# Channel mixers' norms: Newton steps by GpSimd, first guess in one operation on VectorE

## The chip, the cores and the metric

The kernel runs on one core of one Trainium2 chip. The metric is the device time of one execution in microseconds (us); lower is better. Three runs of the kernel before took 1862.06 to 1864.02 us, with a median of 1863.17.

## The reference

A decoder trunk of two layers on 512 tokens of width 1024, all in float32. Each layer is a channel mixer, a token mixer and a second channel mixer, each with a root-mean-square norm in front:

```
h = h + 0.5 * swiglu(rmsnorm(h, ffn_norm_a[i]), ...)
m = rmsnorm(h, mix_norm[i])
h = h + mla_mixer(m, ...)        # layer 0;  nsa_mixer(m, ...) in layer 1
h = h + 0.5 * swiglu(rmsnorm(h, ffn_norm_b[i]), ...)
...
def rmsnorm(x, g):
    y = x32 * lax.rsqrt(jnp.mean(x32 * x32, axis=-1, keepdims=True) + RMS_EPS)
    return y.astype(x.dtype) * g
def swiglu(x, w_gate, w_up, w_down):
    return (jax.nn.silu(x @ w_gate) * (x @ w_up)) @ w_down
```

A final norm stands behind the second layer. The hidden width of the channel mixers is 2816. The latent mixer norms its two latents as well, so there are four channel norms (called a0, b0, a1, b1 here, by layer and place), four others that go through the same code (in front of each token mixer, and of the two latents), and the final one, which has its own code.

## The kernel before

The residual h lies transposed in SBUF: eight tiles of 128 features by 512 tokens. Every product is made of three TensorE passes over a high and a low part of both operands: ScalarE rounds an operand to its high part (L205 in `split`, L176 for a weight slab that is loaded by `slab_ahead`), VectorE subtracts it from the operand for the low part (L206, L178). So each weight slab of 128 x 1024 goes from a DMA through ScalarE and then VectorE before TensorE can use it whole; two buffers named w hold slabs that are ready.

A channel mixer (`ffn`) does its first three hidden tiles f = 0, 1, 2 plainly: for each a gate product into pg and an up product into pu, of 48 matmuls of 256 columns each (L401 to L403: high by high, high by low, low by high, so that the first read of the slab's low part is the third matmul). Behind them the hidden tiles are made with fewer products, from sums of blocks: `combine` reads the residual (ScalarE makes a pair of y halves, L267; VectorE the sums u, L271 to L273; ScalarE and VectorE the parts named four, L205 and L206), and `wsums` makes sums of weight blocks (L372 to L376) and their parts wh and wl.

The norm's factor is not needed for the plain products: the gains are put into x, the products are begun, and the factor, one number for each token, is multiplied in behind the gate product. It is found while TensorE is busy with f = 0 and f = 1: the sums of squares are brought into a column of 128 x 4 (four matmuls pc, L311; in a0 by ScalarE's accumulators, L490), and `rsqrt` finds the inverse root on VectorE by a first guess from the bits of the number (L299, L300) and three Newton steps of three operations (L302 to L304), all on tiles of 128 x 4 in the tile named small. Each operation reads the one before it. Behind the column stand a warm-up of ScalarE's Silu on one of its numbers (L524), four transposes on TensorE that spread it over all partitions (pb, L323), a copy to the tile row (L527), and then the gates (L437 to L439).

The order of the instructions on each engine is not that of the code: the framework's scheduler sets it from its own estimate of when operands are ready, and each engine then works through its queue strictly in that order. GpSimd does not work at these places but for the last additions of squares (L289). `self.to_ffn` is set by `norm_begin` and is true for the four channel norms.

## Time and profile before

| | us |
|---|---|
| median of 3 runs (lowest, highest) | 1863.17 (1862.06, 1864.02) |
| the profiled execution | 1862.05 |
| its span, first to last instruction | 1860.3 |
| TensorE busy | 1845.7 |
| VectorE busy | 1507.4 |
| ScalarE busy | 1064.5 |
| GpSimd busy | 296.7 |

The mean TensorE clock that was granted is 0.999. In the profile PE is TensorE, PEld its weight loads, DVE VectorE, ACT ScalarE, POOL GpSimd and SP SyncE. Rows of a timeline begin with the start and the length in us; a bracket behind a row is the idle time of the engine ahead of it and what ended it. Rows of a group end with busy us, mean ns of one, and idle time ahead of them. A matmul's length is modelled and overlaps the next one's: one of 256 columns starts about 0.112 us behind the other.

The four channel norms' first guesses start at 25.05 (a0), 560.70 (b0), 889.30 (a1) and 1520.81 us (b1).

### The profile page before, as it was taken

The page shows a single profiled execution, that of the slowest core. Times are in us where ns is not written, and L with a number is a line of the kernel's source. Part 1 is how long each engine was busy: PE and PEld are TensorE (multiplying, and loading weights), DVE is VectorE, ACT ScalarE, POOL GpSimd, SP SyncE. Part 2 cuts the span into 40 slices and gives each one's busy share as a digit, 9 for nine tenths or more (in the row PEclk, how much of TensorE's full clock was granted, in tenths as well). Part 3 has the DMA queues.
Part 4 walks back from the last instruction along what each step waited for, and adds up shares of the span by engine and source line. Part 5 has one row for each costly group of instructions (what it writes and reads, how often), then busy time and mean ns, then how long its engine had stood idle before and what let it go on. Part 6 is the DMA issues. An engine that isn't in the chain of part 4 may idle for free.

```text
span 1860.3 us, 37031 instructions
## 1 busy us (share of the span) xinstructions
PE 1845.7 (99%) x14464; PEld 1763.4 (95%) x14464; DVE 1507.4 (81%) x2810; ACT 1064.5 (57%) x1997; POOL 296.7 (16%) x370
## 2 busy tenths in 40 slices
PE   9999999999999999999999999999999999999998
PEld 9999999888889999999999999988888889999997
DVE  8988886688779988886898888666878888888885
ACT  7555553567666555554655545446776865555554
POOL 0000000258830000001000000022666620000000
PEclk9999999999999999999999999999999999999999
DMA  6433331434433433322443332162433133433321
GB/s 238 132 108 103 103 92 48 117 105 103 114 123 112 119 103 109 110 73 72 138 118 110 109 106 81 45 183 82 108 108 103 40 118 116 121 104 107 103 78 69
DMA packets 84351, 196.64 MB, mean 106 GB/s; under 512 B 10944, under 2 KB 38464, under 8 KB 84176
## 3 DMA queue, kind: packets, MB, share of 16 engines
q1 hardware_dynamic: 81664, 191.34, 34.9%
q10 hardware_dynamic: 2512, 2.93, 0.5%
q8 instruction: 114, 1.87, 0.4%
q14 instruction: 61, 0.50, 0.1%
HBM read 178.44 MB, written 2.16 MB: 97 GB/s over the span
## 4 chain that ended last, share of the span: by engine, by line
PE 93%; DVE 3%; ACT 1%; issue 1%; POOL 1%; DMA 0%; ACTq 0%; POOLq 0%; DVEq 0%
PE pd L462 8%; PE pd L464 8%; PE pd L463 8%; PE px L386 6%; PE px L388 6%; PE px L387 5%; PE pg L386 4%; PE pg L388 4%; PE pg L387 4%; PE pq L386 4%; PE pq L388 4%; PE pq L387 4%; PE o L1337 2%; PE pt L1310 2%; PE po L197 2%; PE po L199 2%
## 5 line engine op out<-in xcount | busy, mean ns | idle before, releaser
L462 PE MATMUL pd<-ah,wd 128*128 128x256 f32 x1152 | 318.3, 276 | 0.0
L464 PE MATMUL pd<-ah,wd 128*128 128x256 f32 x1152 | 318.3, 276 | 0.0
L463 PE MATMUL pd<-al,wd 128*128 128x256 f32 x1152 | 318.3, 276 | 0.0
L289 POOL TENSOR_TENSOR s<-s,sq 128x512 f32<-128x512 f32 x38 | 54.7, 1441 | 1050.3 <-ACT sq L285 1050.3
L462 PEld LDWEIGHTS pd<-ah,wd 128*128 128x128 f32 x1152 | 216.3, 188 | 0.0
L464 PEld LDWEIGHTS pd<-ah,wd 128*128 128x128 f32 x1152 | 216.3, 188 | 0.0
L463 PEld LDWEIGHTS pd<-al,wd 128*128 128x128 f32 x1152 | 216.3, 188 | 0.0
L206 DVE TENSOR_TENSOR w<-wr,w 128x1024 fp32r<-128x1024 f32 x72 | 88.2, 1225 | 120.7 <-ACT w L205 120.4
L386 PE MATMUL px<-four,wh 128*128 128x256 f32 x608 | 168.4, 277 | 0.4 <-ACT wh L205 0.2
L388 PE MATMUL px<-four,wl 128*128 128x256 f32 x608 | 168.2, 277 | 0.2 <-DVE wl L206 0.2
L386 PE MATMUL pq<-four,wh 128*128 128x256 f32 x608 | 168.1, 276 | 0.2 <-ACT uq L556 0.2
L387 PE MATMUL px<-four,wh 128*128 128x256 f32 x608 | 168.0, 276 | 0.0
L388 PE MATMUL pq<-four,wl 128*128 128x256 f32 x608 | 167.9, 276 | 0.0
L387 PE MATMUL pq<-four,wh 128*128 128x256 f32 x608 | 167.9, 276 | 0.0
L468 DVE SCALAR_TENSOR_TENSOR h<-pd,h 128x512 f32<-128x512 f32 x216 | 148.3, 686 | 15.4 <-PE pd L464 15.2
L205 ACT ACTIVATE wd<-wdr 128x384 fp32r<-128x384 f32 x192 | 99.2, 519 | 103.8 <-issue 64.6
L176 ACT ACTIVATE w<-wr 128x1024 fp32r<-128x1024 f32 (+3 forms) x89 | 80.8, 908 | 87.5 <-PE pd L464 20.6
L206 DVE TENSOR_TENSOR wd<-wdr,wd 128x384 fp32r<-128x384 f32 x192 | 105.8, 553 | 20.1 <-ACT wd L205 20.0
L178 DVE TENSOR_TENSOR w<-wr,w 128x1024 fp32r<-128x1024 f32 (+3 forms) x75 | 78.3, 1044 | 50.0 <-ACT w L176 49.8
L728 ACT ACTIVATE p<-p,small 128x512 f32<-128x512 f32 (+2 forms) x192 | 106.9, 558 | 19.0 <-DVE small L727 15.3
L386 PEld LDWEIGHTS px<-four,wh 128*128 128x128 f32 x608 | 114.1, 188 | 1.0 <-ACT wh L205 0.4
L388 PEld LDWEIGHTS px<-four,wl 128*128 128x128 f32 x608 | 114.2, 188 | 0.6 <-DVE wl L206 0.6
(379 smaller groups left out, 6264.9 us busy)
## 6 DMA issues: line engine op xcount, KB each, us to landing
wr<-in_w_gu SPq DMA_DIRECT2D x93, 512.0 KB, 3.5
ru<-in_w_gu SPq DMA_DIRECT2D x76, 512.0 KB, 4.3
wdr<-in_w_down SPq DMA_DIRECT2D x192, 192.0 KB, 2.5
wr<-in_w_down SPq DMA_DIRECT2D x24, 256.0 KB, 2.6
wr<-in_mla_w_o SPq DMA_DIRECT2D x8, 512.0 KB, 3.4
th<-btab_d SPq DMA_DIRECT2D x16, 256.0 KB, 3.7
wr<-in_nsa_w_q SPq DMA_DIRECT2D x8, 512.0 KB, 3.8
wr<-in_nsa_w_o SPq DMA_DIRECT2D x8, 512.0 KB, 3.7
```

What stands on the lines that cost most here:

```text
L176: self.copied = nc.scalar.activation(wh[:, m], raw[:, m], AF.Copy)
L178: nc.vector.tensor_tensor(wl[:, m], raw[:, m], f32v(wh[:, m]), op=ALU.subtract)
L205: nc.scalar.activation(hi, src, AF.Copy)
L206: (nc.gpsimd if pool else nc.vector).tensor_tensor(lo, src, f32v(hi), op=ALU.subtract)
L386: mm(out, wh[:, p], xh, start=first and p == 0, stop=False, skip_group_check=True)
L387: mm(out, wh[:, p], xl, start=False, stop=False, skip_group_check=True)
L388: mm(out, wl[:, p], xh, start=False, stop=last and p == KP - 1, skip_group_check=True)
L462: nc.tensor.matmul(o, wh, xh, start=k == b0 and x == 0, stop=False, skip_group_check=True)
L463: nc.tensor.matmul(o, wh, xl, start=False, stop=False, skip_group_check=True)
L464: last = nc.tensor.matmul(o, wl, xh, start=False, stop=k == b1 - 1, skip_group_check=True)
L468: nc.vector.scalar_tensor_tensor(self.h[c], p, 0.5, self.h[c], op0=ALU.mult, op1=ALU.add)
L728: nc.scalar.activation(p_sb[:, :n], p_sb[:, :n], AF.Exp, bias=nm, scale=-1.0, accum_out=sm)
```

## The change

The first guess becomes one operation on VectorE for all eight norms: the bits, read as an integer, times -0.5, plus the constant. For the four channel norms the three Newton steps are done by GpSimd, which has no operation of the form that joins a scalar and two tensors here, so that each step is four operations in place of three. The other four norms keep their steps on VectorE.

```
     def rsqrt(self, y, v, t, psum, n):
         nc.vector.tensor_scalar(v, psum, 1.0 / n, EPS, op0=ALU.mult, op1=ALU.add)
-        self.newton(y, v, t)
+        nc.vector.tensor_scalar(y.bitcast(I32), v.bitcast(I32), -0.5, float(0x5F3759DF), op0=ALU.mult, op1=ALU.add)
+        (self.newton_pool if self.to_ffn else self.newton)(y, v, t)

     def newton(self, y, v, t):
         nc = self.nc
-        nc.vector.tensor_scalar(y.bitcast(I32), v.bitcast(I32), 1, None, op0=ALU.logical_shift_right)
-        nc.vector.tensor_scalar(y.bitcast(I32), y.bitcast(I32), -1.0, float(0x5F3759DF), op0=ALU.mult, op1=ALU.add)
         for _ in range(3):
             nc.vector.scalar_tensor_tensor(t, y, -0.5, v, op0=ALU.mult, op1=ALU.mult)
             nc.vector.tensor_tensor(t, t, y, op=ALU.mult)
             nc.vector.scalar_tensor_tensor(y, t, 1.5, y, op0=ALU.add, op1=ALU.mult)
+
+    def newton_pool(self, y, v, t):
+        e = self.nc.gpsimd
+        for _ in range(3):
+            e.tensor_tensor(t, y, y, op=ALU.mult)
+            e.tensor_tensor(t, t, v, op=ALU.mult)
+            e.tensor_scalar(t, t, -0.5, 1.5, op0=ALU.mult, op1=ALU.add)
+            e.tensor_tensor(y, y, t, op=ALU.mult)
```

Seven lines are added ahead of the rest, so L437 before is L444 in the changed kernel, L524 is L531, and so on. The scheduler orders the queues anew. Away from the eight norms' places, and from what follows a0 up to about 64 us, TensorE's order is the same as before; at three places the following moves matter.

ScalarE at a1: y are the halves that `combine` makes, four its parts, w a weight slab, gains<-small the Silu warm-up that reads the norm's column. Before:

```order
L176 ACTIVATE w<-wr 128x1024
L267 ACTIVATE y<-h_104,gains 128x512
L267 ACTIVATE y<-h_108,gains 128x512
L205 ACTIVATE wh<-s_11777 128x512
L205 ACTIVATE wd<-wdr 128x384 x2
L205 ACTIVATE four<-u 128x1024 x2
L176 ACTIVATE w<-wr 128x1024
L524 ACTIVATE gains<-small 128x1
```

And with the change:

```order
L176 ACTIVATE w<-wr 128x1024
L267 ACTIVATE y<-h_104,gains 128x512
L531 ACTIVATE gains<-small 128x1
L267 ACTIVATE y<-h_108,gains 128x512
L205 ACTIVATE wh<-s_11780 128x512
L205 ACTIVATE wd<-wdr 128x384
L205 ACTIVATE four<-u 128x1024
L205 ACTIVATE wd<-wdr 128x384
L205 ACTIVATE four<-u 128x1024
L176 ACTIVATE w<-wr 128x1024
```

The warm-up, which waits for the column, has moved ahead of the second y, two fours and the slab of the up product of f = 1. In b0 it has likewise moved ahead of one four and the slab of the gate product of f = 2, and in b1 ahead of a y, a four, a y and the slab of the up product of f = 1; in a0 it stands ahead of a y, a four and a slab.

TensorE in a0, where the products of f = 1 end and those of f = 2 begin; pb are the four transposes of the column. Before:

```order
L403 MATMUL pg<-x,w 128x256
L401 MATMUL pg<-x,w 128x256
L323 MATMUL pb<-ident,small 128x128 x4
L402 MATMUL pg<-x,w 128x256
L403 MATMUL pg<-x,w 128x256
```

And with the change:

```order
L409 MATMUL pu<-x,w 128x256
L410 MATMUL pu<-x,w 128x256
L330 MATMUL pb<-ident,small 128x128 x4
L408 MATMUL pg<-x,w 128x256
L409 MATMUL pg<-x,w 128x256
```

The transposes stood behind 28 matmuls of the gate product of f = 2, and now stand ahead of its first. In b0, a1 and b1 they stand where they stood.

VectorE behind the first guess of b0, where the first row is that guess:

```order
L295 TENSOR_SCALAR small<-small 128x4
L206 TENSOR_TENSOR wl<-ru,wh 128x1024
L178 TENSOR_TENSOR w<-wr,w 128x1024
L206 TENSOR_TENSOR four<-u,four 128x1024
L273 TENSOR_TENSOR u<-y,u 128x256
L206 TENSOR_TENSOR wl<-s_7371,wh 128x512
L206 TENSOR_TENSOR four<-u,four 128x1024
L178 TENSOR_TENSOR w<-wr,w 128x1024 x2
```

Before, the steps of Newton's method stood between these rows; now nothing of the norm does, and the second four is the one that reads ScalarE's four behind the warm-up.

## The prediction

> **What bounds the kernel now.** I read the page's busy table first, then the waits, then the stretches around two of the four places where a channel mixer's norm is worked out.

> ```profile
> PE 1845.7 (99%) x14464; PEld 1763.4 (95%) x14464; DVE 1507.4 (81%) x2810; ACT 1064.5 (57%) x1997; POOL 296.7 (16%) x370
> PE pb L323 <- DVE small L304: 1.0, 2, 0.6
> 22.00:36.00 14.00, 13.54 (x120) 13.37 (x119) 12.62 (x29) 13.24 (x21) 0.00 (x0) 1.00 0.73 255
> 886.00:908.00 22.00, 21.83 (x192) 21.63 (x192) 21.05 (x42) 14.80 (x21) 0.00 (x0) 1.00 0.58 182
> ```

> The columns of the stretches are PE, PEld, DVE, ACT and POOL busy. TensorE is the bound: any wait put into its queue is paid in full, and work taken off VectorE is worth only the TensorE waits that it ends. In the second row, the waits, all that TensorE is seen to lose to Newton's last step is 1.0 us, twice, at pb. At the norms GpSimd is idle while VectorE is 90 to 96% full: GpSimd is free there, but VectorE's queue leaves few gaps.

> **What is removed.** A Newton step on VectorE:

> ```profile
> L303 DVE TENSOR_TENSOR small<-small 128x4 f32<-128x4 f32 x24 | 3.8, 160 | 0.4
> 32.24 0.29 PE L323 MATMUL pb<-ident,small 128*128 128x128 f32 x1 [0.46 <-issue]
> 373.70 0.30 PE L323 MATMUL pb<-ident,small 128*128 128x128 f32 x1 [0.59 <-DVE small L304]
> ```

> Forty-four such instructions leave VectorE (10 at each of four channel norms, 1 at each of four other norms), 44 x 0.16 = 7.0 us of a queue that does not bound. Gain: the other norms' chains lose one dependent step of 0.16 plus about 0.04, so 0.2 us each; TensorE waits for three of them (373.70 above is the largest), and I count 0.5 us. The 0.46 us at 32.24 is the channel norm's own wait, replaced below.

> **What a step costs on GpSimd.** The nearest dependent small step is L1146, read by L1147:

> ```profile
> 1328.40 0.22 POOL L1146 TENSOR_TENSOR small<-small,gcmp 128x16 f32<-128x16 f32 x1
> 1328.70 1.05 POOL L1147 TENSOR_TENSOR e<-e,small 128x512 f32<-128x512 f32 x1
> ```

> From start to start 0.30 us, so twelve steps alone take 3.6 us. By the reported span alone it would be 12 x 0.22 = 2.6. [...]

> But it is not alone. Three pairs show GpSimd and VectorE keeping each other out:

> ```profile
> 1226.75 1.30 POOL L968 TENSOR_SCALAR btab<-tb 16x10 f32<-16x10 f32 x1
> 1226.75 1.23 DVE L178 TENSOR_TENSOR w<-wr,w 128x1024 fp32r<-128x1024 f32 x1 [5.01 <-ACT w L176]
> 1228.02 0.37 POOL L968 TENSOR_SCALAR btab<-tb 16x10 f32<-16x10 f32 x2
> 1505.87 1.72 DVE L178 TENSOR_TENSOR w<-wr,w 128x1024 fp32r<-128x1024 f32 x1
> 1507.37 1.38 POOL L289 TENSOR_TENSOR s<-s,sq 128x512 f32<-128x512 f32 x1 [0.86 <-ACT sq L285]
> 1507.51 1.78 DVE L209 SCALAR_TENSOR_TENSOR x<-h,ngains,x 128x512 fp32r<-128x512 f32 x1
> 1510.95 0.74 DVE L209 SCALAR_TENSOR_TENSOR x<-h,ngains,x 128x512 fp32r<-128x512 f32 x1
> ```

> The 16x10 operation of GpSimd, two of which take 0.37 us a little later, takes 1.30 and ends 0.07 us after VectorE's 1.23. In the second pair the roles are turned: L289 comes while L178 runs, gets in when that ends (1507.59), and L209 behind it, 0.74 us alone, takes 1.78. So a step that meets a VectorE operation on two SBUF tensors waits to its end, then goes ahead of the next; and by the time the dependent step is ready, 0.3 us on, that next one is running. While VectorE is full, GpSimd does one Newton step per VectorE operation, like the old interleaving. [...]

> **How long the chains get.** VectorE's operations at these places, all on two SBUF operands, grouped, and then the starts of a0's first and of L299 in each place:

> ```profile
> L206 DVE TENSOR_TENSOR four<-u,four 128x1024 fp32r<-128x1024 f32 x3 | 3.6, 1221 | 1.5 <-ACT four L205 1.5
> L178 DVE TENSOR_TENSOR w<-wr,w 128x1024 fp32r<-128x1024 f32 x2 | 2.4, 1220 | 0.0
> L271 DVE TENSOR_TENSOR u<-y 128x512 f32<-128x512 f32 x2 | 1.4, 684 | 0.0
> L272 DVE TENSOR_TENSOR u<-y,u 128x256 f32<-128x256 f32 x2 | 0.8, 425 | 0.0
> L273 DVE TENSOR_TENSOR u<-y,u 128x256 f32<-128x256 f32 x2 | 0.8, 421 | 0.0
> L206 DVE TENSOR_TENSOR wl<-s,wh 128x512 fp32r<-128x512 f32 x1 | 0.7, 690 | 0.0
> L373 DVE TENSOR_TENSOR ru<-ru,rg 128x512 f32<-128x512 f32 x1 | 0.7, 689 | 0.0
> 25.54 0.68 DVE L271 TENSOR_TENSOR u<-y 128x512 f32<-128x512 f32 x1
> 25.05 0.17 DVE L299 TENSOR_SCALAR small<-small 128x4 int32<-128x4 int32 x1
> 560.70 0.17 DVE L299 TENSOR_SCALAR small<-small 128x4 int32<-128x4 int32 x1
> 889.30 0.16 DVE L299 TENSOR_SCALAR small<-small 128x4 int32<-128x4 int32 x1
> 1520.81 0.16 DVE L299 TENSOR_SCALAR small<-small 128x4 int32<-128x4 int32 x1
> ```

> The new first guess (one operation, 0.17) stands where L299 did. What VectorE then does before it runs dry is in the changed order; it runs dry because the next operation needs ScalarE's, and ScalarE now stands at the Silu warm-up that reads the norm's column (L524, now L531).
> - a0: L271, L272, L178, L273 (0.68 + 0.43 + 1.22 + 0.42 = 2.75) from 25.54: dry at 28.4, five steps done (one before L271). Seven more x 0.30 = 2.1: column at 30.5.
> - b0: L206 wl<-ru, L178, L206 four (1.22 each, all 1024 columns), L273 0.42, wl<-s 0.69 = 4.8 from 560.8: dry at 565.65, five done, column at 567.75.
> - a1: L271, four, L178, L273, L272 = 4.0 from 889.4: dry at 893.4, five done, column at 895.5.
> - b1: L271, L272, four, L178, L273, L272, L373, L273 = 5.5 from 1520.9: dry at 1526.5, eight done, four more: column at 1527.7.

> Before, a0's column came just ahead of the pb of 32.24, and b0's just ahead of a warm-up that is quoted next (568.69): both now come earlier, by some 1.6 and 0.9 us. That is no gain, because what waits for them has been moved earlier still.

> **What waits behind it.** ScalarE works through its queue in order. Its prices, and when TensorE wants the slab:

> ```profile
> 568.69 0.20 ACT L524 ACTIVATE gains<-small 128x1 f32<-128x1 f32 x1 [0.52 <-DVE small L304]
> 568.84 1.06 ACT L176 ACTIVATE w<-wr 128x1024 fp32r<-128x1024 f32 x1
> 890.27 1.32 ACT L267 ACTIVATE y<-h,gains 128x512 f32<-128x512 f32 x2
> 891.50 0.62 ACT L205 ACTIVATE wh<-s 128x512 fp32r<-128x512 f32 x1
> 892.02 0.93 ACT L205 ACTIVATE wd<-wdr 128x384 fp32r<-128x384 f32 x2
> 892.92 1.07 ACT L205 ACTIVATE four<-u 128x1024 fp32r<-128x1024 f32 x1
> 28.44 0.28 PE L401 MATMUL pg<-x,w 128*128 128x256 f32 x1
> 569.18 0.37 PE L401 MATMUL pg<-x,w 128*128 128x256 f32 x1
> 898.90 0.28 PE L401 MATMUL pu<-x,w 128*128 128x256 f32 x1
> 1530.80 0.28 PE L401 MATMUL pu<-x,w 128*128 128x256 f32 x1
> ```

> - a0: pb itself now stands ahead of the matmul of 28.44. TensorE waits there until 30.55: 2.1, less the old 0.46: **+1.65**. Behind it the slabs are in time.
> - b0: column 567.75, warm-up to 568.0, four to 569.0, the slab's high part to 570.05, VectorE's low part (L178) to 571.45. TensorE's third matmul, 0.23 after 569.18, reads the low part: **+2.05**.
> - a1: 895.5, warm-up to 895.8, then y 0.6, wh 0.52, wd 0.45, four 0.97, wd 0.45, four 0.97, slab 1.05 = 5.0: 900.8; VectorE is in its second four until 901.0, low part 902.2; wanted at 899.13: **+3.1**.
> - b1: 1527.7, warm-up to 1528.0, y, four, y, slab = 3.3: 1531.3; VectorE has four and L271 first, low part at 1532.7; wanted at 1531.03: **+1.7**.

> Sum 8.5, less 0.5 for the other norms: +8.0. The profiled execution's span of 1860.3 lies 1.75 under its time of 1862.05; 1862.05 + 8.0 = 1870.05. That execution is the fastest of the runs shown, 1.1 under their median, so the forecast is 1863.17 + 8.0 = **1871**. Transfers I cost at nothing: SyncE's queue loses and gains none, and trades places of down and gate slabs only in two later stretches. TensorE's order between 40 and 64 us changes too; there

> ```profile
> 40.00:64.00 24.00, 23.49 (x194) 1.00 0.28 84
> 100.00:124.00 24.00, 24.00 (x214) 1.00 0.46 130
> ```

> 20 starts are missing against a full stretch, 20 x 0.112 = 2.2 us of waits, which bounds a gain; as much again bounds a loss. I take nothing.

> **The rivals.**
> 1. *Small steps slip between, not slower.* Were GpSimd never held, the columns would come at 28.9, 564.6, 893.2 and 1524.7. Then a0 waits as long as now, b0 saves at most 0.2, b1 nothing, and a1 still loses 0.55 (893.4 + 5.0 + 1.22 = 899.7 against 899.13). With -0.5 for the other norms: about 1863.0. For it: the steps are tiny. Against: the 16x10 operation was tiny too. 21%. Stalls at b0 and b1 begin where the column comes 1.1 and 1.3 us later than here.
> 2. *GpSimd starves until VectorE is dry.* All twelve steps then follow: 3.6 instead of 2.1, 2.1, 2.1 and 1.2, so 1.5 three times and 2.4: +6.6 (a0 0.3 less): 1877.5. Against: L209 had to let L289 go first. 8%.
> 3. *Faster.* Rival 1 with the waits of 40:64 gone as well (-2.2) and the 1.0 of the waits: 1863.17 - 0.5 - 0.2 - 0.46 - 2.2 = 1859.8, at best 1859. Nothing in the moved queues asks for it. 4%.

> **How the numbers follow.** Forecast 67%, rivals 21, 8 and 4%. Under the forecast, starts that TensorE catches up in later waits take up to 3 us off, and longer arbitration puts up to 4 on: its own range is 1867 to 1875. The 8-in-10 range must reach rival 1 and most of rival 2: 1862.5 to 1877.5. 0.2% (3.7 us) is about what a measurement of this kernel can tell from no change: slower by more than that, most of the forecast and rival 2: 0.71; within it: 0.25; faster: 0.04.

> **What would show it.** Right: nearly half of GpSimd's 48 small steps take 0.4 to 1.2 us and end with VectorE's L178, L206, L271; TensorE waits for pb once near 28.4 for about 2 us, and for slabs ("w" by ScalarE, then VectorE) near 569, 899 and 1531; ScalarE's longest idle times stand before the warm-up, released by GpSimd. Wrong: steps of 0.2 us at 0.3 spacing beside a full VectorE (rival 1), or ScalarE that leaves the warm-up before 566, 893.5 and 1526.3.

## The result, and the profile after

The changed kernel takes 1878.21 us (median of 6 executions, 1876.52 to 1882.41) against 1864.10 us for the kernel before (6 executions, 1862.06 to 1865.09): a ratio of 1.0082, with a 95% interval of 1.0068 to 1.0095. It is slower by 14 to 15 us. The forecast was 1871, the range ended at 1877.5. The direction was right, and that all four places lose; the size was not. The profiled execution took 1879.17 us, its span is 1877.3. Two executions of the experiments below were disturbed and count in no median or ratio: one of 6604 us, the profiled one of GpSimd's steps in b0, a1 and b1, so that no rows of that run are shown, and one of 2095.87 us of the first guess with the early warm-up.

The busy table of the page, the waits of TensorE on the norms' columns and weight slabs, and the row of pb in a0, which was shown of before:

```profile
PE 1852.7 (99%) x14464; PEld 1769.8 (94%) x14464; DVE 1504.3 (80%) x2766; ACT 1064.1 (57%) x1997; POOL 317.3 (17%) x418
PE pq L393 <- ACT wh L205: 1.9, 1, 1.9
...
PE pu L410 <- DVE w L178: 1.6, 2, 0.9
PE pb L330 <- POOL small L311: 1.5, 1, 1.5
PE pu L408 <- ACT w L176: 1.5, 1, 1.5
PE pb L330 <- DVE small L303: 1.4, 3, 0.6
PE pg L408 <- ACT w L176: 1.4, 1, 1.4
...
PE pg L410 <- DVE w L178: 0.9, 1, 0.9
30.68 0.32 PE L330 MATMUL pb<-ident,small 128*128 128x128 f32 x1 [1.54 <-POOL small L311]
```

VectorE lost 3 us of busy time and GpSimd took on 21. The waits that were forecast are all there: one for pb on GpSimd's last step, one each for the high part of a slab by ScalarE (L408 after L176) and one each for its low part by VectorE (L410 after L178). At b1 only the low part is late, which is the second of the two under pu L410. The largest wait, pq behind wh, was in no step of the prediction. The three other norms gave nothing back: TensorE waits for them 1.4 us where it was 1.0, so the half microsecond counted as a gain did not come.

**Where the time went, by place.** For this the starts of the same matmul in the two profiles are compared; how far the changed kernel is behind, in us, grows in steps. At the start it is 0.53, behind a0 6.9, ahead of b0 7.25, behind b0 11.4, behind a1 16.0, at the end 16.8. (The two profiled executions lie 1.0 us above and 2.0 below their medians, so these 16.8 stand for the 14.1 between the medians.) So:

| | forecast | lateness gained | of it half clock (below) |
|---|---|---|---|
| a0, from 8 to 150 us | 1.65 | 6.4 | 1.7 |
| b0 | 2.05 | 4.2 | 1.7 |
| a1 | 3.1 | 4.6 | 1.7 |
| b1 | 1.7 | 0.9 | 0 |
| the rest, of it 0.53 ahead of 8 us | -0.5 | 0.7 | 0 |

**GpSimd beside VectorE.** In the timeline, four of GpSimd's operations at b1 (called steps here, as in the prediction; twelve of them make the three Newton steps) with VectorE's operations there, the first three at b0, and ScalarE's stop at a1:

```profile
1537.06 0.57 POOL L308 TENSOR_TENSOR small<-small 128x4 f32<-128x4 f32 x1 [3.38 <-DVE small L295]
...
1538.07 1.03 POOL L310 TENSOR_SCALAR small<-small 128x4 f32<-128x4 f32 x1
1539.18 1.06 POOL L311 TENSOR_TENSOR small<-small 128x4 f32<-128x4 f32 x1
1540.32 0.25 POOL L308 TENSOR_TENSOR small<-small 128x4 f32<-128x4 f32 x1
...
1537.83 1.22 DVE L206 TENSOR_TENSOR four<-u,four 128x1024 fp32r<-128x1024 f32 x1
1538.97 1.22 DVE L178 TENSOR_TENSOR w<-wr,w 128x1024 fp32r<-128x1024 f32 x1
1540.10 0.42 DVE L273 TENSOR_TENSOR u<-y,u 128x256 f32<-128x256 f32 x1
...
568.30 4.32 POOL L308 TENSOR_TENSOR small<-small 128x4 f32<-128x4 f32 x1 [8.60 <-DVE small L295]
572.69 0.20 POOL L309 TENSOR_TENSOR small<-small 128x4 f32<-128x4 f32 x1
572.98 0.19 POOL L310 TENSOR_SCALAR small<-small 128x4 f32<-128x4 f32 x1
...
906.89 0.20 ACT L531 ACTIVATE gains<-small 128x1 f32<-128x1 f32 x1 [4.07 <-POOL small L311]
```

At b1 the steps of 128 x 4 last as long as what is left of VectorE's operation: the one of 1539.18 ends at 1540.24, 0.05 us behind the L178 that ends at 1540.19 (1538.97 + 1.22). One step for each VectorE operation, as forecast: until VectorE runs dry five steps are done at a0, five at a1 and eight at b1, as counted. At b0 it is rival 2: the first step is held past five operations until VectorE runs dry, and eleven steps of 0.28 us follow. The chains from first guess to column come out at 5.0, 7.6, 5.7 and 6.1 us, where 5.45, 7.05, 6.2 and 6.9 were forecast.

**The half clock.** What stands behind the stalls of b0, in four stretches of 3.41 us each, and of a1 and a0's aftermath in the stretch that follows the stall (columns as in the prediction; the number ahead of the DMA share is the granted TensorE clock):

```profile
572.98:576.39 3.41, 3.41 (x31) 3.25 (x30) 0.00 (x0) 0.66 (x2) 1.97 (x10) 1.00 0.26 108
576.39:579.80 3.41, 1.06 (x7) 0.77 (x7) 2.89 (x3) 3.39 (x6) 0.00 (x0) 1.00 0.01 2
579.80:583.21 3.41, 3.41 (x19) 3.41 (x18) 3.41 (x7) 1.65 (x4) 0.00 (x0) 0.51 0.85 268
583.21:586.62 3.41, 3.41 (x31) 3.41 (x31) 1.38 (x4) 0.70 (x2) 0.00 (x0) 0.99 0.27 102
...
914.30:917.71 3.41, 3.41 (x19) 3.41 (x18) 3.41 (x4) 2.37 (x3) 0.00 (x0) 0.51 0.50 154
...
47.33:50.74 3.41, 3.41 (x19) 3.41 (x17) 3.41 (x6) 1.45 (x2) 0.00 (x0) 0.51 0.63 177
```

TensorE is busy and nothing is missing, yet the matmuls of 256 columns start 0.213 us apart instead of 0.113: the granted clock is 0.51 (in the trace's record 0.50 from 47.38 to 50.79, 579.86 to 583.27 and 914.36 to 917.78 us; the stretches quoted begin some 0.05 us ahead of that). One such stretch costs 3.41 x 0.49 = 1.67 us, and there are three: 5.0 of the 16.8. In the kernel before there is none between its first 6 us and its last matmuls: its granted clock is 1.00 from 6.2 to 1856.2 us. Each such stretch lowers the mean granted clock by 0.0009. The mean was 0.996 in the profiled execution and 0.997 or 0.998 in the other five, so these had three at most. The slowest, of 1882.41 us, is the one with 0.998, which leaves room for two at most: something else made it slow, and what is not known.

### The profile page after: what moved, and what is told of

It is laid out like the page before. It is cut to its first block, busy times and chain, and to the rows that moved or that the text cites. A ratio compares the mean times of both kernels' runs of the same rounds, so it can differ in the third digit from the quotient of the medians.

```text
span 1877.3 us, 37046 instructions
## 1 busy us (share of the span) xinstructions
PE 1852.7 (99%) x14464; PEld 1769.8 (94%) x14464; DVE 1504.3 (80%) x2766; ACT 1064.1 (57%) x1997; POOL 317.3 (17%) x418
## 4 chain that ended last, share of the span: by engine, by line
PE 87%; DVE 4%; ACT 2%; POOL 1%; issue 1%; DMA 0%; POOLq 0%; ACTq 0%; DVEq 0%
PE pd L469 8%; PE pd L471 8%; PE pd L470 8%; PE px L395 5%; PE px L393 5%; PE px L394 5%; PE pg L393 4%; PE pg L394 4%; PE pg L395 4%; PE pq L393 4%; PE pq L394 4%; PE pq L395 3%; PE o L1344 2%; PE pt L1317 2%; PE po L197 2%; PE po L199 2%
## 5 line engine op out<-in xcount | busy, mean ns | idle before, releaser
L289 POOL TENSOR_TENSOR s<-s,sq 128x512 f32<-128x512 f32 x38 | 55.7, 1466 | 1010.3 <-ACT sq L285 1010.2
L206 DVE TENSOR_TENSOR w<-wr,w 128x1024 fp32r<-128x1024 f32 x72 | 88.2, 1225 | 120.8 <-ACT w L205 120.4
L205 ACT ACTIVATE wd<-wdr 128x384 fp32r<-128x384 f32 x192 | 99.3, 519 | 110.0 <-issue 68.4
L176 ACT ACTIVATE w<-wr 128x1024 fp32r<-128x1024 f32 (+3 forms) x89 | 80.7, 908 | 89.8 <-PE pd L471 20.0
L206 DVE TENSOR_TENSOR wd<-wdr,wd 128x384 fp32r<-128x384 f32 x192 | 105.2, 551 | 21.7 <-ACT wd L205 21.3
L178 DVE TENSOR_TENSOR w<-wr,w 128x1024 fp32r<-128x1024 f32 (+3 forms) x75 | 78.6, 1049 | 48.9 <-ACT w L176 48.6
L393 PEld LDWEIGHTS pq<-four,wh 128*128 128x128 f32 x608 | 114.5, 188 | 2.1 <-ACT wh L205 2.1
```

The lines of the kernel that those rows point to most:

```text
L176: self.copied = nc.scalar.activation(wh[:, m], raw[:, m], AF.Copy)
L178: nc.vector.tensor_tensor(wl[:, m], raw[:, m], f32v(wh[:, m]), op=ALU.subtract)
L205: nc.scalar.activation(hi, src, AF.Copy)
L206: (nc.gpsimd if pool else nc.vector).tensor_tensor(lo, src, f32v(hi), op=ALU.subtract)
L393: mm(out, wh[:, p], xh, start=first and p == 0, stop=False, skip_group_check=True)
```

## The experiments

Theory A says that the loss goes through ScalarE's queue: it stands at the warm-up until the column is there, and the slabs behind it come late. Theory B says that GpSimd and VectorE, sharing, delay the slabs by themselves. Theory C says that the new order of TensorE behind a0 costs something of its own. The half clock is a fourth term, on top of any stall.

**The first guess alone, and without a0.** The edit of the first run; the second also keeps the old two operations in a0:

```
-        (self.newton_pool if self.to_ffn else self.newton)(y, v, t)
+        self.newton(y, v, t)
```

> The one-operation first guess at all eight norms, with all Newton steps left on VectorE in three operations. If GpSimd's steps cause the loss (theory A, by ScalarE's queue, or theory B, by GpSimd and VectorE keeping each other out), this stands beside the kernel before: 1863.5, within 2 us, and no stretch of half clock on TensorE. If the scheduler's new order of TensorE behind a0 (40 to 64 us) is itself the cause of what is lost there (theory C), a part of it stays, because the order there differs in this kernel too: 1867 to 1870, with waits of 1 to 2 us near 43 and 72 us.

Measured 1865.03 against 1863.47, ratio 1.0007 (0.9998 to 1.0016): no half clock (a mean of 0.999 granted, as before), and 2.0 us gained in lateness at a0, with these waits of TensorE in 36 to 50 us (its order behind a0, from 30 to 71 us, is neither that of the kernel before nor the changed kernel's):

```profile
PE px L395 <- DVE w L206: 1.5, 1, 1.5
PE pq L393 <- ACT wh L205: 0.7, 1, 0.7
```

```
+        if self.place == "a0":
+            nc.vector.tensor_scalar(y.bitcast(I32), v.bitcast(I32), 1, None, op0=ALU.logical_shift_right)
+            nc.vector.tensor_scalar(y.bitcast(I32), y.bitcast(I32), -1.0, float(0x5F3759DF), op0=ALU.mult, op1=ALU.add)
+        else:
             nc.vector.tensor_scalar(y.bitcast(I32), v.bitcast(I32), -0.5, float(0x5F3759DF), op0=ALU.mult, op1=ALU.add)
```

> All Newton steps on VectorE; the one-operation first guess at seven norms, while a0 keeps the old one of two operations. TensorE's order is then the one of the kernel before up to the token mixer. If the 1.3 us that the first guess alone cost come from the new order behind a0, this stands at or below the kernel before: 1863.0, and without the waits of 1.8 and 1.0 us near 40 and 43 us. If the new first guess costs something by itself: 1865 again.

Measured 1863.23 against 1863.39, ratio 1.0000 (0.9991 to 1.0009); lateness gained at a0 0.0, and both waits are gone. One VectorE operation fewer ahead of a0's column leads the scheduler to another order on all engines behind it, and that order costs 2 us in the trace. By medians alone it is not shown, since the two intervals overlap. The first guess itself is worth nothing that can be measured.

**Each place by itself.** GpSimd's steps in a0 alone, and in the other three alone (the choice in `rsqrt` by the name that `norm_begin` is given):

```
+        (self.newton_pool if self.place == "a0" else self.newton)(y, v, t)
```

> GpSimd does Newton's steps in a0 alone; the other three channel norms keep them on VectorE, with the new first guess. TensorE's order is the changed kernel's to the last instruction. The lateness of TensorE in the changed profile grows by 7.1 us to the end of what follows a0: so 1864 + 7 = 1871. If the losses of the four places were alike, it would be 1864 + 15 / 4 = 1868. Half clock: once, near 47 us.

> GpSimd does Newton's steps in b0, a1 and b1, VectorE in a0. By the lateness read from the changed profile (4.5 at b0, 4.6 at a1, 0.9 at b1): 1864 + 10 = 1874, and half clock twice, for 3.4 us each, behind the stalls of b0 and a1. If what is lost at b0 and a1 hangs on what a0 left behind: nearer 1868.

Measured 1870.50, ratio 1.0036 (1.0023 to 1.0048), half clock once, from 46.9 us on; and 1875.57 (median of four executions), ratio 1.0067 (1.0053 to 1.0081). a0 alone costs 7 us. The other three cost at least what was read for them, and do so without a0's help. Less the 1.6 us that the new first guess costs in a0 of the second run, the two come to 17.5 us and the whole change to 14 or 15: each part loses by itself, but the runs don't say how the sum divides.

**The warm-up out of the way.** The Silu warm-up reads the mean of squares, which is there ahead of the first guess; GpSimd's steps stay:

```
-                nc.scalar.activation(self.tiny[:, 4:5], col[:, 0:1], AF.Silu, scale=-1.0)
+                nc.scalar.activation(self.tiny[:, 4:5], self.vtc[:, 0:1], AF.Silu, scale=-1.0)
```

> The changed kernel, but the Silu warm-up of ScalarE reads the mean of squares (there before the first guess) in place of the column that Newton's steps end in. TensorE's, GpSimd's and SyncE's order are the changed kernel's; nothing of ScalarE's but the copy of pb still waits for the column. Theory A (the warm-up stops ScalarE's queue): the stalls at b0, a1 and b1 go, with the half clock behind them (10 us), and at a0 the wait at pb stays (1.2 to 1.7) while VectorE no longer runs dry there: 1865 to 1868. Theory B (the steps' sharing with VectorE delays the slab's low part itself): within 3 us of the changed kernel's 1878. Theory C (TensorE's order behind a0): 5 us stay there: 1869 to 1871.

Measured 1869.04, ratio 1.0030 (1.0019 to 1.0042). At a1 and b1 nothing is lost any more, at b0 0.8, and there is no half clock. ScalarE and TensorE at a1 and b0:

```profile
897.29 0.18 ACT L531 ACTIVATE gains<-small 128x1 f32<-128x1 f32 x1
902.04 1.05 ACT L176 ACTIVATE w<-wr 128x1024 fp32r<-128x1024 f32 x1
...
575.36 0.32 PE L330 MATMUL pb<-ident,small 128*128 128x128 f32 x1 [1.00 <-POOL small L311]
904.00:910.00 6.00, 6.00 (x56) 6.00 (x55) 6.00 (x8) 2.96 (x3) 1.01 (x2) 1.00 0.38 98
```

In the changed kernel ScalarE stood 4.07 us in front of this L531 (906.89, quoted above); here it stands for nothing, and TensorE is full where it was stopped. Yet GpSimd's steps are held more often than in the changed kernel: 35 of the 48 last longer than 0.21 us, there 18. So theory B falls: what is lost at b0, a1 and b1 goes through ScalarE's queue. What is left at b0 is pb itself, 1.0 us. At a0 it is as theory C said: 4.8 us stay, and the time lies in that theory's range. Of them 2.2 are waited at pb (0.46 before), which still stands ahead of the gate product, and some 3 come behind it.

The same for b0, a1 and b1 with a0 left as it was before:

```
-        (self.newton_pool if self.to_ffn else self.newton)(y, v, t)
+        (self.newton_pool if self.to_ffn and self.place != "a0" else self.newton)(y, v, t)
...
-                nc.scalar.activation(self.tiny[:, 4:5], col[:, 0:1], AF.Silu, scale=-1.0)
+                nc.scalar.activation(self.tiny[:, 4:5], (self.vtc if idx else col)[:, 0:1], AF.Silu, scale=-1.0)
```

> GpSimd does Newton's steps in b0, a1 and b1, where the Silu warm-up reads the mean of squares instead of the column; a0 is left as in the kernel before (VectorE, first guess in two operations, warm-up on the column), and TensorE's order is the old one up to the token mixer. If all that is lost at b0, a1 and b1 goes through ScalarE's queue: 1864, at most 1 us of it for a pb of b0 that waits for the column. If GpSimd's steps hold up VectorE's slabs by themselves: 1868 or more. The twin without the early warm-up took 1876.

Measured 1864.68 against 1863.41, ratio 1.0005 (0.9996 to 1.0014). The run with GpSimd's steps at the same three places and the warm-up on the column took 1875.57; it also had the new first guess in a0, which costs 1.3 to 2.0 by the runs above. So some 9 us hang on one operand of one 128 x 1 operation whose result nothing reads.

**The length of the stall.** One Newton step fewer, and one more, by GpSimd:

```
-        for _ in range(3):
+        for _ in range(2):
             e.tensor_tensor(t, y, y, op=ALU.mult)
```

> The changed kernel with the third Newton step left out at the four channel norms (so the factor is less exact): 4 of GpSimd's 12 operations fewer, the last ones, which run free at a pitch of 0.28 us. TensorE's, VectorE's and SyncE's order are the changed kernel's. The column comes 1.1 us earlier at each place. If a stall costs only its own length, the four places give back 1.1, 1.1, 1.1 and 0.8 us: 1878 - 4 = 1874. If the half clock that follows the stalls of 2.2 to 2.9 us is a price of its own (1.7 us for 3.4 us at half clock), and stalls of 1.1 to 1.8 us don't set it off, up to three times 1.7 more come back: 1869.

> The changed kernel with a fourth, superfluous Newton step by GpSimd at the four channel norms; TensorE's, VectorE's and SyncE's order are the changed kernel's. The column comes 1.1 us later at each place. If lateness passes one for one: 1878 + 4.5 = 1882.5. If the half clock is a price of its own, it is now also paid at b1 (stall 2.0 instead of 0.9) or behind pb in a0 (2.8 instead of 1.7): 1884 to 1886. If anything hides the column's lateness: under 1880.

Measured 1873.13, ratio 1.0058 (1.0045 to 1.0070), and 1883.91, ratio 1.0112 (1.0098 to 1.0126): 5.1 us less and 5.7 more for one Newton step (1.1 us of column) at four places. Lateness gained with two, three and four steps: at a0 5.2, 6.4 and 6.0; at b0 1.4, 4.2 and 5.3; at a1 3.7, 4.6 and 7.0; at b1 0.0, 0.9 and 4.9. That is no slope of one for one. At b1 with four steps the added step is not all: GpSimd's first operation was held for 4.79 us until VectorE ran dry, as at b0, where with three steps it took 0.57 (1537.06 above) with the same order of VectorE's queue. The column came 3.1 us later there, not 1.1. With two steps the half clock is gone at b0 but not at a1, with four it is at five stretches, two of them at a1 and one at b1. Two stretches of the kernel with two steps (the stall, and what follows it, at b0 and at a1), then of the one with four (a0's pb, which is no place of half clock though TensorE waits 2.8 us there, and b1 with the held operation in front):

```profile
575.33:578.74 3.41, 2.15 (x16) 1.90 (x16) 3.41 (x5) 2.67 (x5) 0.00 (x0) 1.00 0.13 20
578.74:582.15 3.41, 3.41 (x32) 3.41 (x31) 3.41 (x7) 1.66 (x3) 0.00 (x0) 1.00 0.90 335
906.42:909.83 3.41, 1.91 (x14) 1.51 (x14) 3.41 (x5) 1.59 (x2) 0.00 (x0) 1.00 0.08 10
909.83:913.24 3.41, 3.41 (x19) 3.41 (x18) 3.41 (x4) 2.19 (x3) 0.00 (x0) 0.51 0.41 144
```

```profile
26.26:29.67 3.41, 2.42 (x22) 2.23 (x20) 1.90 (x3) 2.09 (x3) 2.69 (x9) 1.00 1.00 314
29.67:33.09 3.42, 1.75 (x16) 1.75 (x16) 0.93 (x2) 1.77 (x4) 1.18 (x6) 1.00 0.31 119
33.09:36.50 3.41, 3.41 (x33) 3.41 (x32) 3.41 (x5) 2.91 (x6) 0.00 (x0) 1.00 0.01 2
...
1539.00 4.79 POOL L308 TENSOR_TENSOR small<-small 128x4 f32<-128x4 f32 x1 [3.38 <-DVE small L295]
1548.59:1552.00 3.41, 0.82 (x5) 0.41 (x4) 2.79 (x3) 3.41 (x5) 0.00 (x0) 1.00 0.00 0
1552.00:1555.41 3.41, 3.19 (x15) 3.19 (x16) 3.41 (x6) 2.36 (x4) 0.00 (x0) 0.51 0.56 154
```

**The changed kernel again**, for a second profile, with no edit:

> The changed kernel once more, for a second profile. The stalls themselves come from queues in a fixed order, so they are the same to 0.3 us (1.8 at pb of a0, 2.2 near 43, 1.7 and 1.2 at b0, 1.8 and 1.2 at a1, 0.9 at b1). If half clock is decided on a grid of 3.41 us that runs free of the kernel, then every stretch of it ends on one grid within the profile, lasts one grid step, and follows a step in which TensorE idled more than about 1.75 us; which stalls it follows may differ from the first profile's (two to four of them), and the time with it, by 1.7 us each: 1876 to 1881. If half clock is set by the length of one stall alone, it follows the same three stalls again.

It took 1878.49 us, and half clock followed the same three stalls. That by itself does not tell the grid from the stall's length. The ends of the half clock do. By the clock that the traces record they come at 50.79, 583.27 and 917.78 us in the first profile, 532.48 and 866.99 us behind the first of them. Counted in steps of 3.4133 us (866.99 / 254) from the first end, they lie at 156.00 and 254.00 in the first profile, at 156.00 and 254.00 in the second (whose stretches end at 49.39, 581.87 and 916.37 us), at 253.00 with two Newton steps, at 156.00, 255.00 and 441.00 with four: whole steps in all four profiles, wherever the stalls lie.

**a0's aftermath.** pb of a0 behind 30 matmuls of the gate product of f = 2 (28 in the kernel before); then the same with the early warm-up at all four places:

```
+                for k in self.order:
+                    last = self.plain1(w, k, g)
+                    if k == self.order[4]:
+                        spread(col, last)
...
+            with self.tc.issue_after(behind.ins) if behind else nullcontext():
+                pb = self.norm_bcast(col)
```

> The changed kernel, but in a0 the transposes pb stand behind 30 matmuls of the gate product of f = 2, where the kernel before had them behind 28. The wait of 1.7 us at pb goes, and one in part that follows: 1876 if the rest of a0's 6.5 us comes from ScalarE and VectorE that stood still for 3 us, with the half clock near 47 us; 1872 if the place of pb was the cause of what follows it too.

> The changed kernel with both: pb of a0 behind 30 matmuls, and the warm-up on the mean of squares at all four places, so that neither TensorE nor ScalarE stops at a column that is on its way. If these two queues carry the whole loss: 1864 to 1865. If the scheduler's order behind a0 costs 2 us by itself, as the first guess alone showed: 1866.

Measured 1877.34, ratio 1.0074 (1.0061 to 1.0087), and 1865.66, ratio 1.0014 (1.0005 to 1.0023). In the profiles a0 gains 2.2 and 0.6 us of lateness, against 6.4 in the changed kernel and 4.8 with the early warm-up alone. The first of these profiles is its kernel's fastest execution (1874.83; the others up to 1879.73) and has no half clock near 47 us, though TensorE stops there for 2.2 and 1.35 us in a row; they fall into two steps of the grid. The median is 0.9 below the changed kernel's and not 4. More half clock in the other executions doesn't explain it: the median one, of 1877.34 us, was granted 0.998 and the profiled one, with two such stretches, 0.997; only the slowest (0.995) had clearly more. Why the others are slower than the profiled one is open.

With both edits the four places keep GpSimd's steps and some 12 of the 14 us are gone, so most of the loss went through these two queues. 2.2 us stay, nearer to the expectation's 1866 than to its 1864 to 1865, but not for its reason: in the profile only 0.6 of them come at a0. TensorE waits 1.0 at pb of b0 and 0.7 at pb of b1, and the rest is spread.

Four profiles make a table of a0's lateness, all with GpSimd's steps there: pb ahead of the gate product 6.4 and, with the early warm-up, 4.8; pb behind 2.2 and 0.6. So the place of pb, with the order that the scheduler makes for it, is worth 4.2 us, and ScalarE's stop 1.6. That is no better than to 1 us: four more profiles with pb ahead and the warm-up on the column gave 5.1 to 6.0.

**First guess and early warm-up, all on VectorE** (a0 with the old guess):

> The kernel of the row before this one, and the Silu warm-up reads the mean of squares in place of the column, so that ScalarE stops for no Newton step. In the kernel before ScalarE waits 0.5 us at most for the warm-up and TensorE for none of it: so the same, 1863 within 1.5 us. Below 1861 would show that ScalarE's short stops cost TensorE something in the kernel before too.

Measured 1864.55 (median of ten executions), ratio 1.0007 (0.9998 to 1.0017). That is just above what was expected (1861.5 to 1864.5), and TensorE waits 1.1 us for pb of a0. (In the kernel before, ScalarE's longest wait at a warm-up is 1.69 us, at the one of 898.11 in a1, and not 0.5.) The warm-up brings its table load of 1.28 us, and that now stands ahead of a slab in ScalarE's queue; VectorE waits 1.17 us for the slab, and Newton's steps stand behind it in VectorE's. So the early warm-up is not free everywhere: here it cost some 1.3 us at a0.

None of the versions is faster than the kernel before; the nearest, the first guess alone without a0, can't be told from it.

## Why the prediction was wrong in size

- *What bounds, and the mechanism.* Right for b0, a1 and b1: the losses sit behind ScalarE's warm-up, and all but 0.8 us of them go when the warm-up no longer waits. At a0 the wait at pb is there, but the larger part of the loss is behind it.
- *A step on GpSimd.* The free pitch was 0.28 us for a forecast 0.30, and one step per VectorE operation held at three places of four. At b0 the first step starved, which made the column late by 0.6 us more than forecast, not the 1.5 of rival 2. The sign given for it did not come as written: nine of the 48 small steps took 0.4 to 1.2 us, not nearly half, because a step held by one of VectorE's shorter operations (0.4 us) takes only some 0.25. No row of before shows the longer arbitration that the range has up to 4 us for; the steps held by one operation ended 0.05 or 0.06 us behind VectorE, as the one quoted above.
- *The stalls themselves.* The sum was 8.5. Without half clock b0 cost 2.5 (forecast 2.05), a1 2.9 (3.1), b1 0.9 (1.7) and pb in a0 1.1 (1.65): 7.4. The sum was sized well, and b1 was half of its term. Part of that is luck: at b0 the column was later than forecast.
- *The step that failed first:* "any wait put into its queue is paid in full". It is paid in full and then again. In the profiled execution three of the stalls were followed by 3.41 us at half clock, 1.67 us each, 5.0 in all. The prediction has no such term, though its stalls at b0 and a1 (2.05 and 3.1 us) were long enough by the last section's measure, if each fell within one step of the grid. No step of the grid ahead of a half clock was idle throughout: at a1 with two Newton steps, where the clock fell to 0.51, 1.83 us of idleness was enough.
- *The step that failed second:* TensorE's order between 40 and 64 us, "I take nothing", bounded by 2.2 us on either side, and "Behind it the slabs are in time". TensorE's order differs up to 70.7 us of the kernel before, and not to 64. Of a0's 6.4 us, 1.1 are the wait at pb and 1.7 the half clock; 3.6 came behind pb, 1.3 of them later than 70.7. With the early warm-up, and the same order on TensorE, some 3 of these stayed, so the new orders of the queues, and not ScalarE's stop, are most of them. In the changed kernel it reads, with one row of the kernel with the early warm-up last:

```profile
30.66 0.20 ACT L531 ACTIVATE gains<-small 128x1 f32<-128x1 f32 x1 [1.84 <-POOL small L311]
...
31.50 0.69 DVE L271 TENSOR_TENSOR u<-y 128x512 f32<-128x512 f32 x1 [2.89 <-ACT y L267]
...
43.93 0.68 DVE L380 TENSOR_TENSOR ru<-ru,rg 128x512 f32<-128x512 f32 x1
44.64 1.06 ACT L205 ACTIVATE wh<-ru 128x1024 fp32r<-128x1024 f32 x1 [2.17 <-DVE ru L380]
45.75 0.38 PE L393 MATMUL pq<-four,wh 128*128 128x256 f32 x1 [1.92 <-ACT wh L205]
...
42.95 0.69 DVE L380 TENSOR_TENSOR ru<-ru,rg 128x512 f32<-128x512 f32 x1
```

VectorE does ru at 43.93, which in the kernel before it had done at 32.39, and wh and TensorE follow. Its dry 2.89 us are not the reason: with the early warm-up it has no such stop, and does ru at 42.95. The new order has put ru behind the gates. 7.4 + 5.0 + 3.6 is 16.0, the sum of the four places (16.1); how the 3.6 divide between the queues' orders and ScalarE's stop is known only as far as the four values of a0's lateness above tell.
- *The range.* It ended at rival 2, whose mechanism the changed kernel shows at b0 alone, and left the time out by 0.7 us (rival 2's own terms give 1877.8, not 1877.5; that is short too). The bounds were those of the steps, and none of them held what a stall sets off.

## What to carry to other kernels

Before a chain of small steps is given to a slower engine (here 0.20 us for a step alone, against VectorE's 0.16, and four of them in place of three), look up what stands behind its reader in an in-order queue: here the warm-ups' waits for the column went from 2.2 us in all (two places) to 14.5 (four) in ScalarE's queue, with the slabs behind them, and giving them another operand was worth some 9 us. Where TensorE is the bound, as here at 99% busy, price stalls that add up to about 2 us within one step of 3.41 us with another 1.7 for the half clock that followed such stalls in these profiles. Whether a stall falls within one step or is split over two isn't known beforehand, so this is a term with a chance. A shorter chain of estimates can make a scheduler reorder every engine; the price of the new order is to be taken as a term with its own bound.

## What the runs showed of the hardware

GpSimd's first operation at b0 was held past several VectorE operations in all eight profiles that have it there: 4.3 us in five (4.32 in the changed kernel, quoted above), 2.6 in the three with the early warm-up. At b1 it was in two of eight: 4.79 us with four steps, quoted above, and past sixteen operations with pb behind and the early warm-up:

```profile
1524.35 11.21 POOL L308 TENSOR_TENSOR small<-small 128x4 f32<-128x4 f32 x1 [3.38 <-DVE small L295]
```

In all ten it ended within 0.1 us of a moment at which VectorE had run dry or its next operation came later than back to back (in the changed kernel at 572.62, where VectorE's last operation ended at 572.56). Elsewhere, and for every later operation, GpSimd got in behind one VectorE operation (in the changed kernel 0.05 or 0.06 us behind its end at a0, a1 and b1). As b1 shows both with one order of VectorE's queue, that order alone does not decide it; why is open.
